# Rows of a modulation, loaded singly and worked off behind the weight splits of a diffusion layer

## The chip, the cores and the metric

The kernel runs on one core of one Trainium2 chip. The metric is the device time of one execution in microseconds (us), lower is better. Three runs of the kernel before gave 2001.37, 2008.41 and 2005.83 us; the median is 2005.83 us.

## What is computed

One layer of a diffusion backbone in float32: 256 latent tokens (`x`) and 256 context tokens, width 2048. Cut to what matters here:

```python
mod_lat = silu(c) @ w_mod + b_mod          # w_mod: 2048 x 12288
sh1, sc1, g1, sh2, sc2, g2 = split(mod_lat, 6)
u = modulate(rmsnorm(h), sh1, sc1) @ w_in  # context and latent tokens
y_ssm = group_rmsnorm(ssd(u) * silu(z), 4 groups)   # state-space half
y_sc  = rmsnorm(bg * conv(cg * hv))                 # short-convolution half
h = x + g1 * (concat(y_ssm, y_sc) @ w_out)
f = modulate(rmsnorm(h), sh2, sc2)
h = h + g2 * expert_choice_ffn(f, w_router, w_gate, w_up, w_down)  # 16 experts
return rmsnorm(h)
```

The first modulation (`sh1`, `sc1`) is needed at once. The later one (`sh2`, `sc2`, `g1`, `g2`, four vectors of 2048) is needed only after the two halves, and its weights are 4 x 2048 x 2048 numbers, 67 MB.

## The kernel before

Every weight of `w_in` and `w_out` goes through the same step, `split_tile`: SP's queue loads a tile of 512 KB (`raw`, three buffers), ScalarE rounds it to the short float format (`whi`, L89), VectorE subtracts this from the original (`wlo`, L90), and TensorE multiplies three times, high by high, high by low and low by high (L326, L329, L765). `whi` and `wlo` have three buffers each, so TensorE can be at most three tiles behind VectorE. There are 241 such tiles: first some for the first chunk of projections, then from about 200 us on the short convolution's first block, four groups of the state-space half (each with a projection of x in banks `g`, its convolution L389/L391, a scan made of L602 to L630, a projection of z, and a norm), three more blocks of the short convolution, and 64 tiles of `w_out`. Then comes the router, and after it 16 experts, whose 402 MB of weights stream through a ring of buffers of 1 MB (`ebig`, `abig`, `mwt`; L934, L960, L981). Three loads of experts stand in SP's queue already among the tiles of `w_in`.

The later modulation isn't done on TensorE. `mod_lat` takes 512 columns at a time: the 16 row blocks of 128 x 512 (256 KB each) are loaded by POOL's queue (`mraw`, L238), and VectorE multiplies each by its 128 values of `c` and adds it to an accumulator (`macc`, L242 for the first, L244 for the other 15). Four transposes on TensorE (`pc`, L250), a reduction and an addition (L251, L252) make 512 values. 16 such columns make the four vectors, 256 rows in all. A load brings two rows (512 KB) into one of two buffers; the last three columns, in the time of `w_out`, load one row (256 KB) into one of two buffers. The table `MODS` says behind which group, block or pass how many columns are written down.

The order of each engine's instructions is set before the launch by a list scheduler that goes by priority, and priority is the place in the program, shifted by hand: weight tiles 300 places earlier (`AHEAD`), columns 250 later (`LATE`), transposes 50 later (`COLS`), the norms of groups 200 later (`NORM`). On the chip each engine then works its own list strictly in order, so that an instruction which waits holds all behind it.

A norm (`rms_bcast`) sums squares over 128 partitions by a product with ones (`pss`, L543), VectorE and POOL take the power -1/2 (`rc`, L545, L546), and a second product spreads it (`pb`, L549). POOL adds the squares beforehand (`sq`, L638, L639).

Of the kernel before, what the change touches and what calls it, by code (L numbers as in the profile page):

```python
# [17 lines left out]

AHEAD = 300
LATE = 250  # L20
NORM = 200
COLS = 50
# [8 lines left out]
MODS = (1, 1, 1, 1, 1, 1, 1, 0, 0, 0, 1, 1, 1, 1, 1, 1, 3, 0, 0, 0)  # L31
# [3 lines left out]
def layer(ctx: ExitStack, tc: tile.TileContext, x, c, cx, c_ctx, w_mod, b_mod, norm_mix_w, w_in,  # L35
# [27 lines left out]
    def sbank(name="s"):  # L63
        return bank("s", 4, name)
# [10 lines left out]

    def raw_tile():
        return wp.tile([P, 2, 512], F32, name="raw", tag="raw", bufs=3)

    def split_tile(src, k0, c0, n, kn):

        with tc.high_priority(offset=ahead[0]):
# [8 lines left out]
            nc.vector.tensor_tensor(lv, wv, hv.bitcast(F32), op=OP.subtract)  # L90
        return hv, lv

# [140 lines left out]
    def mod_lat(c0, dst, pool, kn, bias, paired):  # L233

        acc = pool.tile([P, 512], F32, name="macc", tag="macc", bufs=1)
        for k0 in range(0, KT, kn):
            w = pool.tile([P, kn, 512], F32, name="mraw", tag="mraw", bufs=2)
            nc.gpsimd.dma_start(w, w_mod.rearrange("(k p) c -> p k c", p=P)[:, k0:k0 + kn, c0:c0 + 512])  # L238
            for j in range(kn):
                cs = csl[:, k0 + j:k0 + j + 1]  # L240
                if k0 + j == 0:
                    nc.vector.tensor_scalar(acc, w[:, j], cs, None, op0=OP.mult)  # L242
                else:
                    nc.vector.scalar_tensor_tensor(acc, w[:, j], cs, acc, op0=OP.mult, op1=OP.add)  # L244
        with tc.high_priority(offset=-COLS):
            pc = sbank("pc")
            av = acc.rearrange("p (b c i) -> p b i c", b=2, i=2)
            for j in range(4):
                src = av[:, j // 2, j % 2] if paired else acc[:, P * j:P * j + P]
                nc.tensor.transpose(pc[:, P * j:P * j + P], src, ident)  # L250
            nc.vector.tensor_reduce(dst, pc.rearrange("p (j k) -> p j k", j=4), axis=mybir.AxisListType.X, op=OP.add)  # L251
            nc.vector.tensor_tensor(dst, dst, bias, op=OP.add)  # L252

# [224 lines left out]
    def sc_block(j, gp, dst):  # L478
# [7 lines left out]
        if j:  # L486
            mods_late(8 + 2 * j, gp)
# [30 lines left out]

    mods = const.tile([P, 4, KT], F32, name="mods")
    sh2, G, g1c, g2c = (mods[:, i] for i in range(4))
    late = [(j, q) for j in range(4) for q in range(4)]

    def mod_late(pool=None, kn=2):
        with tc.high_priority(offset=-LATE):
            j, q = late.pop(0)
            dst = mods[:, j, 4 * q:4 * q + 4]
            c0 = (3, 4, 2, 5)[j] * D + 512 * q
            bias = pcol[:, 1 + j, 4 * q:4 * q + 4] if j < 2 else bcol[:, c0 // P:c0 // P + 4]  # L530
            mod_lat(c0, dst, pool or mp, kn, bias, j < 2)
            if j == 1:
                nc.vector.scalar_tensor_tensor(dst, dst, 1.0, nffn[:, 4 * q:4 * q + 4], op0=OP.add, op1=OP.mult)

    def mods_late(i, pool=None, kn=2):
        for _ in range(MODS[i]):
            mod_late(pool, kn)

    def rms_bcast(sq, n):

        pss = sbank("pss")
        for t in range(2):
            nc.tensor.matmul(pss[:, t:t + 1], sq[:, P * t:P * t + P], ones[:, 0:1], start=True, stop=True)  # L543
        rc = const.tile([P, 2], F32, name="rc", tag="rc", bufs=2)
        nc.vector.tensor_scalar(rc, pss[:, 0:2], 1.0 / n, EPS, op0=OP.mult, op1=OP.add)  # L545
        nc.gpsimd.tensor_tensor(rc, rc, mhalf[:, 0:2], op=OP.pow)  # L546
        pb = sbank("pb")
        for t in range(2):
            nc.tensor.matmul(pb[:, P * t:P * t + P], rc[:, t:t + 1].to_broadcast([P, P]), ident, start=True, stop=True)  # L549
        return pb[:, 0:L]  # L550
# [103 lines left out]
    def gate_norm(g):  # L654
# [7 lines left out]
        with tc.high_priority(offset=-NORM):  # L662
            rb = rms_bcast(squares(y32[g]), 512)
            normed(y32[g], rb, nssm[:, 4 * g:4 * g + 4])

    for g in range(NG):
        ssd_group(g)
        mods_late(2 * g)
        gate_norm(g)
        mods_late(2 * g + 1)  # L670
    ssdg.close()
    ssd.close()
    mpool.close()
# [13 lines left out]
    sums = gp.tile([P, L], F32, name="scs")  # L687
    yt = None
    for j in range(1, 4):
# [9 lines left out]
        mods_late(9 + 2 * j, gp)  # L699
    rb = rms_bcast(sums, D)  # L700
    for j in range(4):
        normed(ysc[j], rb, nsc[:, 4 * j:4 * j + 4])
# [4 lines left out]
    g2r = hp_.tile([P, 512], F32, name="g2r")  # L707
# [4 lines left out]
    for j in range(4):  # L712
        ysplit(ysc[j], 4 + j)
    ypool.close()
# [329 lines left out]
```

## Time and profile before

| | us |
|---|---|
| median of three runs | 2005.83 |
| the profiled execution | 1996.63 |
| its span, first to last instruction | 1994.8 |
| TensorE busy | 1651.4 |
| VectorE busy | 900.3 |
| ScalarE busy | 516.6 |
| POOL busy | 143.9 |

Until about 1060 us TensorE is nearly always busy; from then on the 16 DMA engines are, at 420 GB/s, to near the end. Busy time of TensorE is modelled for pipelined matmuls, so a stretch in which it is busy throughout may still hold slow ones; the granted clock stands beside it (1.00 is 2.4 GHz, and at 1.2 GHz it reads 0.50). "Idle before" and "waited for" name what ended a wait last.

### The profile page before, as it was taken

To read this page: it belongs to the slowest core of one execution; us is meant where nothing else is said; L and a number is where in the kernel's file an instruction comes from. 1 tells how busy PE (TensorE), PEld (TensorE's weight loads), DVE (VectorE), ACT (ScalarE), POOL (GpSimd) and SP (SyncE) were. 2 spreads that over 40 slices of the span, in tenths; PEclk is the share of its full clock that TensorE was granted. 3 is DMA by queue.
4 is the path that set the end of the run, shared out by engine and by line. 5 is a ranking of instruction groups with operands and counts; after the bars stand their busy time and mean duration, and the time that the engine had idled before them with its cause. 6 is when DMAs were issued, how large, how long until landed. Compare 5 with 4: busy or idle time off the path is not lost.

```text
span 1994.8 us, 25507 instructions
## 1 busy us (share of the span) xinstructions
PE 1651.4 (83%) x10318; PEld 991.2 (50%) x10318; DVE 900.3 (45%) x1390; ACT 516.6 (26%) x850; POOL 143.9 (7%) x209
## 2 busy tenths in 40 slices
PE   7999999999899989989988766676667676767775
PEld 5677997868698989877872111111111111111122
DVE  2458975867888777886743101111101111111113
ACT  4322574373657333433320000000000000000002
POOL 1001000101121212111200000000000000000000
PEclk9999999999999989999999899989899989888998
DMA  9965654736476888797888999999999999999997
GB/s 354 405 233 145 207 148 115 234 110 218 150 232 197 306 313 290 260 319 260 271 310 365 420 420 420 420 420 420 420 420 420 420 420 420 420 421 420 420 420 276
DMA packets 178086, 641.12 MB, mean 321 GB/s; under 512 B 17549, under 2 KB 50594, under 8 KB 128944
## 3 DMA queue, kind: packets, MB, share of 16 engines
q1 hardware_dynamic: 158496, 570.20, 74.2%
q0 software_dynamic: 19184, 68.24, 11.0%
q8 instruction: 81, 1.33, 0.3%
q10 hardware_dynamic: 288, 1.05, 0.1%
q14 instruction: 37, 0.30, 0.0%
HBM read 637.34 MB, written 2.10 MB: 321 GB/s over the span
## 4 chain that ended last, share of the span: by engine, by line
DMA 58%; PE 22%; issue 9%; DVE 8%; ACT 1%; SPq 1%; POOL 1%; DVEq 0%; POOLq 0%; ACTq 0%
DMA abig<-in_w_up_dram 16%; DMA mwt<-in_w_up_dram 9%; PE g L329 9%; DMA mraw<-in_w_mod_dram 9%; DMA abig<-in_w_down_dram 8%; PE g L326 6%; DMA mwt<-in_w_down_dram 6%; DMA ebig<-in_w_up_dram 5%; DVE macc L244 3%; DVE wlo L90 2%; DMA raw<-in_w_in_dram 2%; DMA ebig<-in_w_down_dram 1%; DMA raw<-in_w_out_dram 1%; PE pm L216 1%; PE s L329 1%
## 5 line engine op out<-in xcount | busy, mean ns | idle before, releaser
L329 PE MATMUL g<-abig,whi 128*128 128x256 f32 x2048 | 376.3, 287 | 15.2 <-ACT whi L89 7.5
L89 ACT CAST whi<-raw 128x1024 fp32r<-128x1024 f32 x241 | 253.9, 1054 | 381.7 <-DMA raw<-in_w_in_dram 92.5
L90 DVE TENSOR_TENSOR wlo<-raw,whi 128x1024 fp32r<-128x1024 f32 x241 | 293.6, 1221 | 102.7 <-ACT whi L89 100.2
L329 PEld LDWEIGHTS g<-abig,whi 128*128 128x128 f32 x2048 | 319.8, 194 | 21.3 <-issue 11.8
L329 PE MATMUL g<-abig,wlo 128*128 128x256 f32 x1024 | 285.7, 288 | 4.7 <-DVE wlo L90 4.6
L940 PE MATMUL gu<-abig,xe 128*32 128x512 f32 x1088 | 202.2, 625 | 78.6 <-DMA abig<-in_w_up_dram 58.1
L244 DVE SCALAR_TENSOR_TENSOR macc<-mraw,csl,macc 128x512 f32<-128x512 f32 x240 | 185.6, 773 | 85.6 <-DMA mraw<-in_w_mod_dram 83.6
L326 PE MATMUL g<-abig,whi 128*128 128x512 f32 (+1 forms) x672 | 213.2, 397 | 2.4 <-ACT abig L310 2.0
L945 DVE SCALAR_TENSOR_TENSOR hid<-hid,gu 64x512 f32<-64x512 f32 x16 | 10.9, 679 | 444.9 <-ACT hid L944 444.9
L944 ACT ACTIVATE hid<-gu 64x512 f32<-64x512 f32 x16 | 9.4, 590 | 765.9 <-PE gu L940 765.9
L329 PEld LDWEIGHTS g<-abig,wlo 128*128 128x128 f32 x1024 | 194.5, 194 | 9.1 <-DVE wlo L90 6.9
L940 PE MATMUL gu<-mwt,xe 128*32 128x512 f32 x616 | 122.5, 629 | 49.9 <-DMA mwt<-in_w_up_dram 37.1
L765 PE MATMUL g<-whi,abig 128*128 128x512 f32 (+1 forms) x640 | 157.6, 350 | 2.6 <-DVE htmp L772 2.2
L940 PEld LDWEIGHTS gu<-abig,xe 128*32 128x32 f32 x1088 | 38.4, 110 | 230.4 <-DMA abig<-in_w_up_dram 101.9
L238 POOL DMA_DIRECT2D mraw<-in_w_mod_dram x152 | 101.1, 665 | 681.0 <-DVE macc L244 475.6
L326 PEld LDWEIGHTS g<-abig,whi 128*128 128x128 f32 (+1 forms) x672 | 122.4, 185 | 38.4 <-issue 8.3
L326 PE MATMUL g<-abig,wlo 128*128 128x512 f32 (+1 forms) x336 | 130.6, 394 | 0.0
L765 PEld LDWEIGHTS g<-whi,abig 128*128 128x128 f32 x640 | 112.5, 191 | 18.8 <-issue 2.5
L974 DVE TENSOR_TENSOR ebig<-ebig,g 128x512 f32<-128x512 f32 x112 | 71.7, 683 | 81.7 <-PE g L970 81.5
L765 PE MATMUL g<-wlo,abig 128*128 128x512 f32 (+1 forms) x320 | 103.3, 355 | 5.0 <-DVE wlo L90 4.5
L963 PE MATMUL yd<-abig,hidT 128*32 128x512 f32 x512 | 74.2, 673 | 34.4 <-DMA abig<-in_w_down_dram 30.2
L940 PE MATMUL gu<-ebig,xe 128*32 128x512 f32 x344 | 73.4, 636 | 28.5 <-DMA ebig<-in_w_up_dram 18.9
(317 smaller groups left out, 1565.5 us busy)
## 6 DMA issues: line engine op xcount, KB each, us to landing
raw<-in_w_in_dram SPq DMA_DIRECT2D x177, 512.0 KB, 4.7
abig<-in_w_up_dram SPq DMA_DIRECT2D x68, 1024.0 KB, 19.9
abig<-in_w_gate_dram SPq DMA_DIRECT2D x68, 1024.0 KB, 19.9
abig<-in_w_down_dram SPq DMA_DIRECT2D x64, 1024.0 KB, 19.9
mraw<-in_w_mod_dram POOLq DMA_DIRECT2D x104, 512.0 KB, 5.0
mwt<-in_w_down_dram SPq DMA_DIRECT2D x43, 1024.0 KB, 19.9
mwt<-in_w_gate_dram SPq DMA_DIRECT2D x39, 1024.0 KB, 19.9
mwt<-in_w_up_dram SPq DMA_DIRECT2D x38, 1024.0 KB, 19.9
```

The source lines that it names most:

```text
L89: nc.scalar.copy(hv, wv)
L90: nc.vector.tensor_tensor(lv, wv, hv.bitcast(F32), op=OP.subtract)
L216: nc.tensor.matmul(pm[32 * q:32 * q + 32, o:o + n], cst[:, k], w[:, k - k0], start=(k < 4), stop=(k >= KT - 4), skip_group_check=True)
L238: nc.gpsimd.dma_start(w, w_mod.rearrange("(k p) c -> p k c", p=P)[:, k0:k0 + kn, c0:c0 + 512])
L244: nc.vector.scalar_tensor_tensor(acc, w[:, j], cs, acc, op0=OP.mult, op1=OP.add)
L326: nc.tensor.matmul(banks[ct][0:ncol], st, a[q][:, kk], start=beg, stop=end)
L329: nc.tensor.matmul(banks[ct // 2][0:ncol, o:o + L], st, a[q][:, kk, L:2 * L], start=beg and ct % 2 == 0, stop=end, skip_group_check=True)
L765: nc.tensor.matmul(ob[nn * t + m], yy[i][:, kk, P * t:P * t + P], w[:, j, n * m:n * m + n], start=(kt == order[0] and pi == 0), stop=(kt = ...
L940: nc.tensor.matmul(gu[32 * q:32 * q + 32], xe[:, k], wt[q // 2][:, 1024 * kk + 512 * (q % 2):1024 * kk + 512 * (q % 2) + 512], start=(k == ...
L945: nc.vector.scalar_tensor_tensor(hid, hid, 1.0, gu[0:64], op0=OP.add, op1=OP.mult)
L963: nc.tensor.matmul(yd[32 * q:32 * q + 32], hidT[:, j, 32 * c2:32 * c2 + 32], t[:, 512 * q:512 * q + 512], start=(kt == 0), stop=(kt == FF ...
L974: nc.vector.tensor_tensor(av, h[:, t, 512 * q:512 * q + 512] if e_ == 0 else av, pc[q], op=OP.add)
```

## The change

The change does five things. A counter (`tick`) goes up by one with each weight tile, and work can be put off by a number of tiles (`at_tick`). The function for a column becomes a generator that yields after every row; behind each tile's subtraction the tile gives out 1.30 rows on average until 192 rows are done (three vectors), and 1.05 in the time of `w_out` until 256. A row is always one load of 256 KB, into one of four buffers (the same memory as two of 512 KB). The reduction after a column's transposes is put off by two tiles. The sums of a norm are put off by three tiles and their spreading by two more; what follows from the last norm, the split of the short convolution's result and the preparation of the router are put off with it. The sum of squares goes into one of the four row buffers, the hand-set shifts of priority are gone, and the memory pool of the rows stays open until the experts.

```diff
-MODS = (1, 1, 1, 1, 1, 1, 1, 0, 0, 0, 1, 1, 1, 1, 1, 1, 3, 0, 0, 0)
+RATE, RATE_OUT = 130, 105
...
-            nc.vector.tensor_tensor(lv, wv, hv.bitcast(F32), op=OP.subtract)
+            sub = nc.vector.tensor_tensor(lv, wv, hv.bitcast(F32), op=OP.subtract)
+        tick[0] += 1
+        with tc.issue_after(sub.ins):
+            for x in sorted(y for y in due if y[0] <= tick[0]):
+                due.remove(x)
+                x[2]()
+            if pace[0]:
+                pace[0]()
...
-            w = pool.tile([P, kn, 512], F32, name="mraw", tag="mraw", bufs=2)
-            nc.gpsimd.dma_start(w, w_mod.rearrange("(k p) c -> p k c", p=P)[:, k0:k0 + kn, c0:c0 + 512])
...
+                for k in range(KT):
+                    w = mp.tile([P, 512], F32, name="mraw", tag="mraw", bufs=4)
+                    nc.gpsimd.dma_start(w, w_mod[P * k:P * k + P, c0:c0 + 512])
+                    cs = csl[:, k:k + 1]
+                    if k == 0:
+                        nc.vector.tensor_scalar(acc, w, cs, None, op0=OP.mult)
+                    else:
+                        nc.vector.scalar_tensor_tensor(acc, w, cs, acc, op0=OP.mult, op1=OP.add)
+                    if k < KT - 1:
+                        yield
...
+                at_tick(2, fin)
+                yield
...
+    def rms_bcast(sq, n, then):
+
+        def sums():
+            pss = sbank("pss")
...
+            def spread():
+                pb = sbank("pb")
...
+                then(pb[:, 0:L])
+            at_tick(2, spread)
+        at_tick(3, sums)
...
-        nc.gpsimd.tensor_tensor(sq[0][:, 0], sq[0][:, 0], sq[0][:, 1], op=OP.add)
-        return sq[0][:, 0]
+        out = mp.tile([P, 512], F32, name="sqs", tag="mraw", bufs=4)[:, 0:L]
+        nc.gpsimd.tensor_tensor(out, sq[0][:, 0], sq[0][:, 1], op=OP.add)
+        return out
...
+    rms_bcast(sums, D, finish_sc)
...
+    at_tick(6, prepare)
```

Three places in the order of instructions. First TensorE in the first pass of `w_out`, where the short convolution's sums (`pss`) and their spreading (`pb`) stand among the weight products, before:

```order
L765 MATMUL g<-whi,abig 128x512 x2
L250 MATMUL pc<-ident,macc 128x128
L543 MATMUL pss<-ones,scs 128x1 x2
L250 MATMUL pc<-ident,macc 128x128 x3
L549 MATMUL pb<-ident,rc 128x128 x2
L726 MATMUL pt<-ident,mods 128x128 x12
L765 MATMUL g<-whi,abig 128x512 x2
```

and now:

```order
L402 MATMUL pc<-ident,macc 128x128 x4
L574 MATMUL pss<-ones,g2r 128x1 x2
L802 MATMUL g<-whi,abig 128x512 x2
L802 MATMUL g<-wlo,abig 128x512 x2
L802 MATMUL g<-whi,abig 128x512 x4
L802 MATMUL g<-wlo,abig 128x512 x2
L802 MATMUL g<-whi,abig 128x512 x4
L802 MATMUL g<-wlo,abig 128x512 x2
L802 MATMUL g<-whi,abig 128x512 x4
L802 MATMUL g<-wlo,abig 128x512 x2
L802 MATMUL g<-whi,abig 128x512 x6
L802 MATMUL g<-wlo,abig 128x512 x2
```

Between sums and spreading there was no weight product; now two and a half tiles of them stand there (the rows go on with `whi` x1 and then `pb`).

Second VectorE in the second group of the state-space half, at the convolution that frees the banks `g` (`cvt` is its scratch, `macc` a row of the modulation), before:

```order
L90 TENSOR_TENSOR wlo<-raw,whi 128x1024
L244 SCALAR_TENSOR_TENSOR macc<-mraw,csl,macc 128x512
L389 SCALAR_TENSOR_TENSOR cvt<-g,col_124,cvt 128x255
L244 SCALAR_TENSOR_TENSOR macc<-mraw,csl,macc 128x512
L391 SCALAR_TENSOR_TENSOR cvt<-g,col_124,cvt 128x255
L389 SCALAR_TENSOR_TENSOR cvt<-g,col_124,cvt 128x4x63
L244 SCALAR_TENSOR_TENSOR macc<-mraw,csl,macc 128x512
L391 SCALAR_TENSOR_TENSOR cvt<-g,col_124,cvt 128x4x63
L244 SCALAR_TENSOR_TENSOR macc<-mraw,csl,macc 128x512
L545 TENSOR_SCALAR rc<-pss 128x2
L90 TENSOR_TENSOR wlo<-raw,whi 128x1024
```

and now (`W`, `ce` and `py` belong to the scan of the group before):

```order
L441 SCALAR_TENSOR_TENSOR cvt<-g,col_124,cvt 128x255
L443 SCALAR_TENSOR_TENSOR cvt<-g,col_124,cvt 128x255
L441 SCALAR_TENSOR_TENSOR cvt<-g,col_124,cvt 128x4x63
L653 TENSOR_TENSOR W<-W,cbm 128x1536
L443 SCALAR_TENSOR_TENSOR cvt<-g,col_124,cvt 128x4x63
L96 TENSOR_TENSOR wlo<-raw,whi 128x1024
L655 TENSOR_TENSOR W<-W 128x4x128
L652 TENSOR_TENSOR ce<-ce,CT 128x1024
L441 SCALAR_TENSOR_TENSOR cvt<-g,col_124,cvt 128x255
L443 SCALAR_TENSOR_TENSOR cvt<-g,col_124,cvt 128x255
L441 SCALAR_TENSOR_TENSOR cvt<-g,col_124,cvt 128x4x63
```

The rows of the modulation no longer stand between the pieces of that convolution. They come later, at places in runs, of which the longest is this one in the same group:

```order
L96 TENSOR_TENSOR wlo<-raw,whi 128x1024
L395 SCALAR_TENSOR_TENSOR macc<-mraw,csl,macc 128x512 x9
L652 TENSOR_TENSOR ce<-ce,CT 128x1024
L395 SCALAR_TENSOR_TENSOR macc<-mraw,csl,macc 128x512
L96 TENSOR_TENSOR wlo<-raw,whi 128x1024
```

Ten rows stand there between two subtractions; in the order before the longest run, in the third group, is of ten as well.

Third POOL's queue around the squares (`sq`) of the first group, before:

```order
L238 DMA mraw<-in_w_mod_dram 128x2x512 x2
L638 TENSOR_TENSOR sq<-sq 128x512
L639 TENSOR_TENSOR sq<-sq 128x256
L238 DMA mraw<-in_w_mod_dram 128x2x512 x6
L546 TENSOR_TENSOR rc<-rc,mhalf 128x2
```

and now:

```order
L390 DMA mraw<-in_w_mod_dram 128x512 x35
L674 TENSOR_TENSOR sq<-sq 128x512
L676 TENSOR_TENSOR sqs<-sq 128x256
L390 DMA mraw<-in_w_mod_dram 128x512 x4
L577 TENSOR_TENSOR rc<-rc,mhalf 128x2
```

Before the first squares 10 loads with 20 rows were issued, now 42 loads with 42 rows; behind them the loads still wait for the squares.

## Rows read from the trace of the kernel before

**Rows 1.** Busy by stretch: PE, PEld, DVE, ACT, POOL; then clock, DMA share, GB/s.

```profile
225.00:340.00 115.00, 115.00 (x803) 101.11 (x802) 81.08 (x112) 74.12 (x137) 2.52 (x2) 1.00 0.49 139
340.00:565.00 225.00, 213.09 (x1238) 173.66 (x1237) 177.60 (x258) 116.62 (x226) 36.88 (x45) 0.98 0.59 183
565.00:640.00 75.00, 74.05 (x568) 65.25 (x568) 60.64 (x78) 51.37 (x105) 9.47 (x12) 1.00 0.68 206
640.00:810.00 170.00, 157.88 (x1267) 154.91 (x1266) 133.78 (x170) 67.22 (x77) 36.78 (x46) 0.97 0.87 294
810.00:1012.00 202.00, 188.25 (x1011) 158.01 (x1010) 150.21 (x189) 77.91 (x90) 37.67 (x64) 0.98 0.83 280
```

**Rows 2.** The chain of waits where the experts begin: start, us, what.

```profile
1058.94 3.67 PE gu L940 x32
1062.61 9.48 DMA ebig<-in_w_down_dram
```

**Rows 3.** Busy by stretch, as in the first group, around the first expert.

```profile
1045.00:1050.00 5.00, 3.70 (x8) 1.44 (x8) 4.73 (x21) 0.58 (x1) 0.00 (x0) 1.00 1.01 419
1055.00:1060.00 5.00, 3.67 (x26) 1.34 (x22) 2.02 (x6) 0.58 (x1) 0.00 (x0) 0.78 0.18 72
1065.00:1070.00 5.00, 5.00 (x52) 1.54 (x48) 0.00 (x0) 0.00 (x0) 0.00 (x0) 1.00 1.01 421
```

**Rows 4.** What TensorE waited for, 340 to 1012 us: total, times, longest.

```profile
PE g L329 <- ACT whi L89: 7.5, 2, 6.3
PE g L329 <- DVE cvt L391: 6.8, 4, 2.5
PE g L329 <- DVE wlo L90: 4.6, 8, 1.3
PE g L765 <- DVE wlo L90: 4.5, 6, 1.1
PE pc L250 <- DVE macc L244: 4.2, 4, 2.4
PE py L629 <- DVE W L619: 2.5, 2, 2.1
PE g L765 <- DVE htmp L772: 2.2, 1, 2.2
PE pb L549 <- POOL rc L546: 1.4, 2, 1.0
```

**Rows 5.** Costliest groups: busy, mean ns | idle before, and what ended it.

```profile
L244 DVE SCALAR_TENSOR_TENSOR macc<-mraw,csl,macc 128x512 f32<-128x512 f32 x240 | 185.6, 773 | 85.6 <-DMA mraw<-in_w_mod_dram 83.6
L238 POOL DMA_DIRECT2D mraw<-in_w_mod_dram x152 | 101.1, 665 | 681.0 <-DVE macc L244 475.6
```

**Rows 6.** What VectorE waited for, 870 to 1012 us: total, times, longest.

```profile
DVE macc L244 <- DMA mraw<-in_w_mod_dram: 34.2, 27, 3.2
```

**Rows 7.** Loads of two rows, 640 to 870 us, issue to landing.

```profile
DMA to landing us min/median/max: 4.1/5.5/9.4
```

**Rows 8.** Loads of one row, 870 to 1012 us, issue to landing.

```profile
DMA to landing us min/median/max: 2.9/4.1/6.7
```

**Rows 9.** POOL's DMA queue, 640 to 810, then 875 to 1006 us: packets, MB, share.

```profile
q0 software_dynamic: 5034, 18.33, 33.8%
...
q0 software_dynamic: 3596, 11.79, 27.8%
```

**Rows 10.** Busy by stretch, as in the first group, around two long waits.

```profile
725.00:735.00 10.00, 3.65 (x22) 3.15 (x22) 1.82 (x2) 2.38 (x3) 0.00 (x0) 0.72 0.79 304
735.00:745.00 10.00, 10.00 (x68) 10.00 (x67) 8.46 (x11) 2.85 (x3) 2.17 (x3) 0.76 0.91 298
865.00:870.00 5.00, 1.62 (x12) 0.95 (x10) 3.74 (x7) 2.09 (x2) 0.81 (x2) 0.94 0.58 216
```

**Rows 11.** SP's queue, 700 to 745 us: start, us, issue.

```profile
713.48 0.46 SPq L934 DMA_DIRECT2D ebig<-in_w_gate_dram  x1
...
716.39 25.23 SPq L84 DMA_DIRECT2D raw<-in_w_in_dram  x7
```

**Rows 12.** What POOL waited for, whole span: total, times, longest.

```profile
POOL sq L638 <- ACT sq L637: 121.4, 5, 114.4
```

More of the change, by code (lines that the diff above doesn't have):

```diff
@@ L19 @@
 AHEAD = 300
-LATE = 250
-NORM = 200
-COLS = 50
 URGENT = 200
@@ L377, in layer, with mod_rows_to, pace_, fn @@
+    steps = mod_rows()
+    n_rows, owed = [0], [0]
+    def mod_rows_to(n):
+        while n_rows[0] < n and next(steps, 0) is None:
+            n_rows[0] += 1
+    def pace_(rate, top):
+        def fn():
+            owed[0] += rate
+            mod_rows_to(min(top, n_rows[0] + owed[0] // 100))
+            owed[0] %= 100
+        return fn
+    pace[0] = pace_(RATE, 12 * KT)
     ssd = ExitStack()
@@ L517, in layer @@
     gp = ssdg.enter_context(tc.tile_pool(name="ssdg", bufs=1, reuse_waits="tile"))
[L521 to L550, printed above, removed]
+    def rms_bcast(sq, n, then):
+        def sums():
+            pss = sbank("pss")
+            for t in range(2):
+                nc.tensor.matmul(pss[:, t:t + 1], sq[:, P * t:P * t + P], ones[:, 0:1], start=True, stop=True)
+            rc = const.tile([P, 2], F32, name="rc", tag="rc", bufs=2)
+            nc.vector.tensor_scalar(rc, pss[:, 0:2], 1.0 / n, EPS, op0=OP.mult, op1=OP.add)
+            nc.gpsimd.tensor_tensor(rc, rc, mhalf[:, 0:2], op=OP.pow)
+            def spread():
+                pb = sbank("pb")
+                for t in range(2):
+                    nc.tensor.matmul(pb[:, P * t:P * t + P], rc[:, t:t + 1].to_broadcast([P, P]), ident, start=True,
+                                     stop=True)
+                then(pb[:, 0:L])
+            at_tick(2, spread)
+        at_tick(3, sums)
     y_hi, y_lo = [None] * 4, [None] * 4
@@ L685, in layer @@
     gp = sp = scx.enter_context(tc.tile_pool(name="sc", bufs=1, reuse_waits="tile"))
-    sums = gp.tile([P, L], F32, name="scs")
+    g2r = hp_.tile([P, 512], F32, name="g2r")
+    sums = g2r[:, 0:L]
     yt = None
@@ L698, in layer @@
                 nc.gpsimd.tensor_tensor(sums, sums, sq, op=OP.add)
[L699 to L702, printed above, removed]
+    mod_rows_to(12 * KT)
+    pace[0] = pace_(RATE_OUT, 16 * KT)
     scx.close()
@@ L743, in layer, with prepare @@
-    nc.vector.tensor_copy(shw, psb[:, 0:NE])
+    shw = hp_.tile([P, NE], F32, name="shw")
+    g1 = []
+    def prepare():
+        g1p = rpool.enter_context(tc.tile_pool(name="g1p", bufs=1, reuse_waits="tile"))
+        g1b = g1p.tile([P, D], F32, name="g1b")
+        g1.append(g1b)
+        for q in range(4):
+            pt = sbank("pt")
+            for j in range(4):
+                k = 4 * q + j
+                nc.tensor.matmul(pt[:, P * j:P * j + P], g1c[:, k:k + 1].to_broadcast([P, P]), ident, start=True, stop=True)
+            nc.scalar.copy(g1b[:, 512 * q:512 * q + 512], pt)
+        nc.gpsimd.memset(gwr, 0.0)
+        for i in range(2):
+            nc.sync.dma_start(wr.rearrange("p (b i) e -> p i b e", i=2)[:, i],
+                              w_router.rearrange("(b p i) e -> p i b e", p=P, i=2)[:, i])
+        psb = sbank("psb")
+        for k in range(KT):
+            nc.tensor.matmul(psb[0:1, 0:NE], sh2[:, k:k + 1], wr[:, k], start=(k == 0), stop=(k == KT - 1))
+        nc.vector.tensor_tensor(wr, wr, G.rearrange("p (k o) -> p k o", o=1).to_broadcast([P, KT, NE]), op=OP.mult)
+        srow = rp.tile([1, NE], F32, name="srow")
+        nc.vector.tensor_copy(srow, psb[0:1, 0:NE])
+        psb = sbank("psb")
+        nc.tensor.matmul(psb[:, 0:NE], ones[0:1, 0:P], srow, start=True, stop=True)
+        nc.vector.tensor_copy(shw, psb[:, 0:NE])
@@ L747, in layer @@
     pq, pl, ns = None, None, 0
-    for pi_, (c0, cn) in enumerate(passes):
-        mods_late(16 + pi_, rp, 1)
+    for c0, cn in passes:
         n = min(cn, 512)
@@ L809, in layer @@
             ns += 1
+    mod_rows_to(16 * KT)
+    flush()
+    rpool.close()
+    rq = rpool.enter_context(tc.tile_pool(name="rq", bufs=1, reuse_waits="tile"))
     rh = const.tile([P, 2], F32, name="rh")
@@ L876, in layer @@
     rpool.close()
+    mpool.close()
     wpool.close()
```

94 lines of the change are left out of this document (40 added, 54 removed).

## The prediction

> **What bounds the kernel now.** I read the busy times by stretch first, then the chain of waits at the end, then what TensorE waits for, and last the row loads. The stretches show TensorE busy 115.00 of 115 us between 225 and 340, and 213.09 of 225, 74.05 of 75, 157.88 of 170 and 188.25 of 202 us after it, while the DMA share stays under 0.9 and VectorE is busy for 70 to 81% of the time [rows 1]. So up to the router the kernel is bound by TensorE, and all that can be won there is its idle time and its slow clock. The idle time from 340 to 1012 us is 11.91 + 0.95 + 12.12 + 13.75 = 38.7 us. The granted clock of those stretches, 0.98, 1.00, 0.97 and 0.98, costs 0.02 x 225 + 0.03 x 170 + 0.02 x 202 = 13.6 us more. The ceiling of any gain is thus about 52 us.
>
> What follows the router moves as a block. The first expert's products begin at 1058.94 us, and from 1062.61 on the chain is a row of weight loads up to the end [rows 2]. Before that the DMA engines run out of work: their share falls from 1.01 to 0.18 between 1055 and 1060 us and is back at 1.01 at 1065 [rows 3]. The buffers for experts are full by then, and the next load needs a product that frees one. So a microsecond won before the router is a microsecond of the whole, and one lost likewise.
>
> **The change part by part.** The work is the same: 256 rows of 0.773 us on VectorE [rows 5], the same transposes and products, the same bytes. 152 loads become 256; a load keeps POOL for 0.665 us [rows 5], which is 69 us more on an engine that is busy for 37 of 225 or 170 us [rows 1] and off the path. What changes is when a row can be had, and what stands in front of what.
>
> *Supply of rows, (a).* VectorE sat idle for 83.6 us before rows whose load had not landed [rows 5], 34.2 us of it between 870 and 1012 [rows 6]. While it waits, the subtractions behind it wait too, and TensorE has at most three tiles in hand. What the buffers can give follows from issue, landing and use. Two buffers of two rows: 0.665 + 5.5 [rows 7] + 2 x 0.773 = 7.7 us for four rows, 1.9 us a row. Two buffers of one row, in the time of `w_out`: 0.665 + 4.1 [rows 8] + 0.773 = 5.5 us for two, 2.8 us a row. Four buffers of one row: 5.5 us for four, 1.4 us a row. The need: a tile takes TensorE 24 matmuls of 157.88 / 1267 = 0.125 us [rows 1], 3.0 us, and the order now puts 74 rows behind 52 tiles of the three later blocks, so one in 2.1 us; in `w_out` it is 73 rows behind 64 tiles in 202 us before, one in 2.8. So the old buffers could just supply that or not quite, and the new ones have a third to spare. TensorE's waits for `wlo` and for the last row ahead of the transposes are 4.6 + 4.5 + 4.2 = 13.3 us [rows 4]. All of it could go, or none if they come from the sheer number of instructions; I take two thirds, 8.9 us, since the waits for rows are most frequent where these waits are.
>
> *Sums given out later, (b).* At the short convolution's sums TensorE stood idle for 3.4 of 5 us [rows 10], with the order showing sums, transposes and spreading back to back. Now two and a half tiles (7.5 us) stand between. Most of that idle time is the wait for the last row (2.4), counted in (a); the wait for the power on POOL is 1.4 us in all [rows 4]. I take 1.0. What is late next: the 16 multiplications and the splits behind the spreading still stand ahead of the next subtractions on VectorE, and there TensorE may wait for a microsecond or two again, which I count in (f).
>
> *Order on VectorE, (c).* Waits for a convolution that frees the banks (6.8), for `W` (2.5) and for `htmp` (2.2) make 11.5 us [rows 4]. In the order, rows between the 66th and the 125th subtraction, which is the time of groups 1 to 3, fall from 94 to 62, because 42 instead of 20 are already done by then; those between the pieces of the convolution are gone. That frees 32 x 0.773 = 25 us on VectorE in a stretch where it was busy for 177.60 of 225. But ScalarE stands in those chains as well, and nothing was done for it. I take a third, 3.8 us (0 to 11.5).
>
> *The tiles behind the expert loads, (d).* At 713.48 us SP issues three loads of 1 MB for experts, and the next weight tile only at 716.39 [rows 11]; TensorE then waits 6.3 of the 7.5 us that it waits for `whi` [rows 4]. The three loads stand at the same place of SP's queue in both orders. Whether TensorE gets through depends on how many split tiles it has in hand, which is 3 x 3.0 = 9 us when VectorE isn't late, as it was here. I take half, 3.7 us (0 to 7.5).
>
> *The clock, (e).* The granted clock falls to the lower level behind the longer waits: 0.72 and 0.76 in the two stretches around that wait [rows 10]. Fewer waits mean fewer falls; I take half of 13.6, 6.8 us.
>
> *New waits, (f).* Between 225 and 340 us no row was worked off, since POOL stood for 114.4 us before the squares of the first group and the loads behind them stood with it [rows 12]. Now 22 more rows fall there or before, 17 us on a VectorE that is busy for 81 of 115 us [rows 1]; it still fits, with little to spare. The sum of squares takes one of the four row buffers until its product is done. And rows still come in runs, below. I take 5 us, bounds 0 to 25.
>
> The sum: 8.9 + 1.0 + 3.8 + 3.7 + 6.8 - 5 = 19.2 us. Against the profiled execution (1996.63 us, of which 1.8 around the span of 1994.8) that gives 1977.4. The three runs lie above it, 2001 to 2008, and no row says where these 9 us are; I take the gain from their median: 2005.8 - 19.2 = 1986.6, so 1987.
>
> One rule speaks against the split of the loads. POOL's queue moved 18.33 MB of two-row loads with 33.8% of 170 us, 3.13 us a MB, and 11.79 MB, nearly all in one-row loads, with 27.8% of 131 us, 3.09 us a MB [rows 9]: single rows cost the DMA engines nothing more. The Trainium skill (DMA: Bandwidth & Descriptors, "Anatomy of one DMA") gives a load from POOL a fixed 2.0 us and the rest by its bytes, and "Measured" there advises batches of 1 MiB. By that, as an estimate from the page, 256 KB would take 2.6 us where 512 KB take 3.2, 1.6 times as much for a MB; the trace does not agree.
>
> **The rivals.** *Rows still come in runs (A).* "One or two rows behind each tile" doesn't hold in the groups: POOL still stands before each group's squares with the loads behind it [rows 12], and the order shows runs of up to ten rows between two subtractions, as before. Then (c) and (d) don't come, and half of (e): 19.2 - 3.8 - 3.7 - 3.4 = 8.3 us, 1997.5. The order speaks for it; the smaller number of rows in the groups against it.
>
> *Nothing to be measured (B).* VectorE still has the same instructions, and each wait removed lets TensorE run into the next one. If of (a) to (e) only half comes, with 8 us of new waits, the gain is 24.2 / 2 - 8 = 4.1 us: 2002. For it: VectorE is at 79% in the groups even without its waits [rows 1].
>
> *Runs that starve TensorE (C), slower.* In a run the first four rows are there, the others come as buffers allow: with one buffer held by the squares, 5.5 / 3 = 1.8 us each. Ten rows then take 4 x 0.773 + 6 x 1.8 = 14 us, in which no tile is split, and TensorE has 9 us in hand. It waits 5 us, and its clock falls, some 2.5 us more (a quarter of 10 us, as in the stretch with 0.76 [rows 10]). The order has five runs of five rows or more in the groups. If all cost this, it is 37 us; against (a) to (e) without (c), 20.4, that is 17 us slower: 2022. It decides once the runs cost more than these 20 us. Against it: the runs before, up to ten rows too, left no wait over 2.5 us in that stretch [rows 4], because TensorE has the scan's products there.
>
> *Single rows cost DMA time (D).* If a one-row load took 1.6 times the DMA time of its bytes, the share of 33.8% would grow by 0.2, the DMA share of that stretch from 0.87 [rows 1] to 1.07, and the 170 us by 12: 2005.8 - 19.2 + 12 = 1999. The cost by MB [rows 9] speaks against it. The rule of the skill is what this rival would be.
>
> **How the numbers follow.** A measurement of this kernel can tell a change of 0.3%, 6 us. The forecast has 0.48, with its own range of 1974 to 1997; A 0.18, B 0.16, C 0.15, D 0.03. Faster by more than 6 us: the forecast, A and D, less 0.02 of A and D that lie within 6 us: 0.67. Within 0.3%: B and those 0.02, 0.18. Slower: C, 0.15. The range is 1966 to 2011: the lower end is the ceiling of 52 us less a quarter that will stay, the upper a C in which two or three runs cost the full price.
>
> **What would show it.** Right for (a): VectorE's idle time before rows falls from 83.6 us to under 35, and TensorE's waits for `wlo` and the last row from 13.3 to about 4. (b): no wait of TensorE for the power. (c): the wait for the convolution falls from 6.8 to about 4. (d): the wait for `whi` after the three expert loads is under 4 us. (e): the clock of the stretches up to the router reads 0.98 or more throughout. The first expert's products begin 15 to 25 us earlier, and from there to the end it takes the same time as before; if that distance changes, the reading of the end as a block is wrong. Wrong in all: TensorE's idle time before the router at 35 us or more, or waits of 3 us and more for `wlo` in the groups behind runs of rows, which would be C.

## The result, and the profile after

The changed kernel takes 1977.8 us (median of 4 runs, 1976.4 to 1980.8), the kernel before 2003.6 in the same series (2000.4 to 2008.4). The ratio is 0.9871 [0.9845, 0.9897]: it is 25.8 us faster. The forecast was 1987 us, in a range of 1966 to 2011, and faster with a chance of 0.67. A second series of the same two kernels gave 1978.5 and 2004.1 us, 0.9872 [0.9849, 0.9895]. The profiled execution of the changed kernel has a span of 1974.6 us, against 1994.8.

The two spans differ by 20.2 us, the medians by 25.8. The traced execution of before took 1996.63 us and lies below every timed run of it (1997.5 to 2010.7 over all series), so what follows explains the 20 us between the traces. For the other 5 or 6 there is no trace.

First the busy time by stretch of the changed kernel (start and end in us; length and busy time of PE, PEld, DVE, ACT, POOL with their counts; then granted clock, DMA share, GB/s). It answers to [rows 1].

```profile
225.00:340.00 115.00, 115.00 (x782) 104.00 (x780) 91.14 (x130) 54.42 (x78) 14.83 (x28) 1.00 0.68 210
340.00:565.00 225.00, 216.89 (x1285) 173.94 (x1284) 171.34 (x243) 136.25 (x284) 38.61 (x59) 0.98 0.49 150
565.00:640.00 75.00, 75.00 (x582) 66.58 (x581) 60.13 (x67) 53.23 (x109) 14.22 (x20) 1.00 0.63 196
640.00:803.00 163.00, 154.43 (x1262) 153.00 (x1261) 137.06 (x179) 64.44 (x71) 51.46 (x83) 0.98 0.92 316
803.00:1012.00 209.00, 200.51 (x1137) 167.91 (x1136) 155.24 (x195) 82.12 (x98) 44.54 (x79) 1.00 0.86 298
```

TensorE's idle time from 340 to 1012 us is now 8.1 + 0 + 8.6 + 8.5 = 25.2 us, where it was 38.7. The clock costs 0.02 x 225 + 0.02 x 163 = 7.8 us, where it was 13.6 (it is printed to two decimals, so each of these products can be off by about 1 us). Those two give 13.5 + 5.8 = 19.3 us. Where the experts begin, the chain of waits (start, us, what), against [rows 2]:

```profile
1037.37 16.50 PE gu L982 x128
```

That is 21.6 us earlier than 1058.94. From there to the end it takes 937.2 us, before 935.9. Next what TensorE waited for from 340 to 1012 us (total, times, longest), against [rows 4]:

```profile
PE g L328 <- ACT whi L95: 7.0, 2, 4.9
PE g L802 <- ACT whi L95: 3.8, 3, 2.1
PE g L802 <- DVE wlo L96: 2.8, 3, 1.7
PE py L665 <- DVE W L655: 2.2, 1, 2.2
PE g L328 <- DVE cvt L443: 2.1, 2, 1.3
PE g L325 <- DVE zt L697: 1.8, 1, 1.8
PE g L328 <- DVE wlo L96: 1.8, 3, 1.0
PE py L665 <- DVE ce L652: 1.5, 2, 0.8
PE g L802 <- DVE htmp L809: 1.0, 1, 1.0
```

The waits for `wlo` have halved, those for the last row ahead of the transposes (4.2 us) and for the power (1.4 us) are gone, that for the convolution fell from 6.8 to 2.1. The wait for `whi` has grown, from 7.5 to 10.8. The rows on VectorE and their loads on POOL, from the page's costliest groups (busy, mean ns | idle before, and what ended it), against [rows 5]:

```profile
L395 DVE SCALAR_TENSOR_TENSOR macc<-mraw,csl,macc 128x512 f32<-128x512 f32 x240 | 185.7, 774 | 31.5 <-DMA mraw<-in_w_mod_dram 29.3
...
L390 POOL DMA_DIRECT2D mraw<-in_w_mod_dram x256 | 137.7, 538 | 586.4 <-DVE macc L395 318.0
```

VectorE's idle time before rows fell from 83.6 to 29.3 us with the duration of a row unchanged. Part of it came back in another place: its idle time before subtractions that wait for ScalarE's rounding rose from 100.2 to 131.0 us. VectorE now waits more for tiles and less for rows.

### The profile page after: what moved, and what is told of

It reads as the page before. It is cut to its first block, busy times and chain, and to the rows that moved or that the text cites. A ratio compares the mean times of both kernels' runs of the same rounds, so it can differ in the third digit from the quotient of the medians.

```text
span 1974.6 us, 25811 instructions
## 1 busy us (share of the span) xinstructions
PE 1645.2 (83%) x10318; PEld 985.4 (50%) x10318; DVE 905.5 (46%) x1390; ACT 514.9 (26%) x850; POOL 184.0 (9%) x313
## 3 DMA queue, kind: packets, MB, share of 16 engines
q0 software_dynamic: 20848, 68.25, 10.1%
q10 hardware_dynamic: 288, 1.05, 0.1%
## 4 chain that ended last, share of the span: by engine, by line
DMA 52%; PE 31%; issue 8%; DVE 4%; ACT 2%; POOL 2%; SPq 1%; POOLq 0%; DVEq 0%; ACTq 0%
DMA abig<-in_w_up_dram 15%; PE g L325 11%; DMA mwt<-in_w_up_dram 9%; DMA abig<-in_w_down_dram 8%; PE g L328 6%; DMA mwt<-in_w_down_dram 6%; PE g L802 5%; DMA ebig<-in_w_up_dram 5%; DMA mraw<-in_w_mod_dram 5%; DMA raw<-in_w_in_dram 1%; PE pm L236 1%; PE s L328 1%; POOL mraw L390 1%; PE gu L982 1%; DMA ebig<-in_w_down_dram 1%
## 5 line engine op out<-in xcount | busy, mean ns | idle before, releaser
L96 DVE TENSOR_TENSOR wlo<-raw,whi 128x1024 fp32r<-128x1024 f32 x241 | 295.6, 1229 | 132.1 <-ACT whi L95 131.0
L395 DVE SCALAR_TENSOR_TENSOR macc<-mraw,csl,macc 128x512 f32<-128x512 f32 x240 | 185.7, 774 | 31.5 <-DMA mraw<-in_w_mod_dram 29.3
L390 POOL DMA_DIRECT2D mraw<-in_w_mod_dram x256 | 137.7, 538 | 586.4 <-DVE macc L395 318.0
```

The costliest lines, as they stand in the source:

```text
L96: sub = nc.vector.tensor_tensor(lv, wv, hv.bitcast(F32), op=OP.subtract)
L390: nc.gpsimd.dma_start(w, w_mod[P * k:P * k + P, c0:c0 + 512])
L395: nc.vector.scalar_tensor_tensor(acc, w, cs, acc, op0=OP.mult, op1=OP.add)
```

## The experiments

Theory S: the supply of rows (single loads in four buffers) brings most of it. Its rivals: N, the late sums; R, the rows' new places; later B (bandwidth), O, P and Q for single stretches; these letters are not those of the prediction's rivals. Every kernel was timed against the kernel before, in 4 to 12 runs.

| kernel | median us | ratio to before, interval | first product of `w_out` | from there to the first expert | from there to the end |
|---|---|---|---|---|---|
| before | 2003.6 | | 815.2 | 243.8 | 935.9 |
| changed | 1977.8 | 0.9871 [0.9845, 0.9897] | 803.7 | 233.7 | 937.2 |
| e1 two-row loads | 2009.4 | 1.0026 [1.0015, 1.0037] | 826.5 | 236.2 | 937.2 |
| e2 sums at once | 1976.7 | 0.9853 [0.9833, 0.9874] | 803.9 | 233.8 | 937.2 |
| e3 before, four singles | 1990.2 | 0.9924 [0.9908, 0.9940] | 809.6 | 245.3 | 937.6 |
| e4 rows not loaded | 1970.3 | 0.9840 [0.9820, 0.9860] | 806.5 | 224.5 | 936.9 |
| e5 expert loads spaced | 1977.5 | 0.9867 [0.9842, 0.9893] | 801.0 | 238.4 | 936.5 |
| e6 rows in the groups | 1983.7 | 0.9891 [0.9875, 0.9907] | 815.9 | 232.6 | 937.2 |
| e10 rows earlier | 1988.4 | 0.9931 [0.9909, 0.9953] | 820.5 | 231.0 | 937.4 |
| e11 router products late | 1979.6 | 0.9890 [0.9869, 0.9910] | 807.0 | 233.4 | 936.0 |
| e12 one pair in `w_out` | 1995.1 | 0.9955 [0.9940, 0.9971] | 804.1 | 252.3 | 937.5 |

The last three columns are from one trace each, in us. The traced executions took 1996.6 (before), 1976.4 (changed), 2001.8 (e1), 1994.4 (e3) and 1987.4 us (e6), so that a column can be some us off what the medians say.

**e1, two rows to a load.** The bytes held are the same, in two buffers instead of four. The sum of squares goes back into `sq`, as before, and takes no row buffer (not shown).

```diff
-                    w = mp.tile([P, 512], F32, name="mraw", tag="mraw", bufs=4)
-                    nc.gpsimd.dma_start(w, w_mod[P * k:P * k + P, c0:c0 + 512])
+                    if k % 2 == 0:
+                        w2 = mp.tile([P, 2, 512], F32, name="mraw", tag="mraw", bufs=2)
+                        nc.gpsimd.dma_start(w2, ...[:, k:k + 2, c0:c0 + 512])
+                    w = w2[:, k % 2]
...
```

> The changed kernel (1977.8 us, against 2003.6 before) with its rows loaded two at a time into two buffers of two rows, as before; the order and the late sums stay. Theory S (the supply of rows brings most: VectorE no longer stands before rows, so splits come in time and the clock stays up): VectorE's idle time before rows goes back from 29 us to 70 or more, TensorE's waits for wlo and for the last row from 4.6 us to about 13, and the time to 1988 to 1996 us. Rival N (the late sums bring most) and rival R (rows worked off earlier and fewer of them in the groups bring most): 1976 to 1983 us, whatever VectorE waits.

2009.4 us: the whole gain goes, and 4.5 us of the time before with it. VectorE's idle time before rows is 58.9 us, less than the 70 expected. What TensorE waited for in that kernel from 340 to 840 us (columns as above):

```profile
PE g L328 <- DVE wlo L96: 8.1, 13, 1.3
PE py L667 <- DVE W L657: 6.9, 1, 6.9
PE g L328 <- ACT whi L95: 5.4, 2, 4.2
PE pss L576 <- POOL sq L677: 5.2, 2, 4.5
PE pb L584 <- POOL rc L579: 2.9, 2, 2.6
```

The waits for `wlo` are back, and with them three that neither kernel had at this size: `W` in the last group, the squares and the power on POOL. N and R predicted no change and fail: the new order with the old loads is slower than the old order. By the table the loss lies ahead of `w_out` (22.8 us), and only 2.5 us in it. That a load of two needs both halves of a buffer free, so that rows come in bursts, is the likely reason; it wasn't tested alone.

**e2, sums at once.**

```diff
-            at_tick(2, spread)
-        at_tick(3, sums)
+            spread()
+        sums()
```

> The changed kernel with the norm's sums and their spreading given out at once instead of three and two tiles later. S and R: TensorE waits about 1.5 us for the power on POOL again and a few more us for the last row and the squares, 1978 to 1982 us. N: the late sums are what keeps VectorE's and TensorE's queues running past the norms, and most of the 26 us go: 1988 to 1998 us.

1976.7 us, not to be told from the changed kernel. N falls. The waits for the power don't even come back; with the rows supplied, no step waits for the norms either way.

**e3, four single-row buffers in the kernel before.**

```diff
-            w = pool.tile([P, kn, 512], F32, name="mraw", tag="mraw", bufs=2)
+            w = pool.tile([P, kn, 512], F32, name="mraw", tag="mraw", bufs=nb)
...
-    def mods_late(i, pool=None, kn=2):
+    def mods_late(i, pool=None, kn=1, nb=4):
```

> The kernel before with its rows up to w_out loaded singly into four buffers, and nothing else (in the time of w_out it had two single-row buffers and keeps them). S: VectorE's idle time before rows falls from 83.6 to about 50 us (the 34 us of w_out stay), TensorE's waits for wlo and the last row up to the router fall by half, and 6 to 12 of the 26 us come: 1991 to 1998 us. N and R: less than 3 us, 2000 to 2004.

1990.2 us: 14.8 us faster than before (2004.9 in that series), by an edit of the rows ahead of `w_out` alone. Its trace took only 2.3 us less than that of before: `w_out` begins 5.6 us earlier, and 1.5 us are lost behind that. Where the other 12 us of the medians are won, no trace shows. Its row group on the page:

```profile
L244 DVE SCALAR_TENSOR_TENSOR macc<-mraw,csl,macc 128x512 f32<-128x512 f32 x240 | 184.9, 771 | 59.1 <-DMA mraw<-in_w_mod_dram 56.8
```

26.8 us of VectorE's idle time have gone, close to the 34 expected. In the table `w_out` is as slow as before, since its two buffers stayed. TensorE's wait for the convolution stays too (340 to 840 us):

```profile
PE g L329 <- DVE cvt L391: 7.3, 4, 2.8
```

**e6, rows back in the groups.**

```diff
-    pace[0] = pace_(RATE, 12 * KT)
...
     for g in range(NG):
+        pace[0] = pace_(250 if g == 0 else 196, 12 * KT)
         ssd_group(g)
...
+        pace[0] = pace_(108, 12 * KT)
         sc_block(j, gp, ...)
```

> The changed kernel with its rows paced as they lay before: none ahead of the first group, 20 in it, 94 in groups 1 to 3, 78 in the later blocks; single loads, four buffers and late sums stay. S: VectorE works off 31 rows more in the groups, but from buffers that keep up: 1977 to 1984 us, and the convolution's wait up by 2 to 4 us. R: the 32 rows (25 us of VectorE) are what made TensorE wait in the groups: the waits from 340 to 565 us go back up by 5 us or more and the time to 1986 to 1995 us. N: 1976 to 1980.

1983.7 us, 4 us given back by the ratios and 6 by the medians: the upper end of S, and below R. The stretch where it happens (columns as in the first table of stretches) and the wait, from 340 to 840 us:

```profile
565.00:640.00 75.00, 67.17 (x488) 58.01 (x487) 63.50 (x84) 46.59 (x98) 15.32 (x29) 0.93 0.69 225
```

```profile
PE py L664 <- DVE W L654: 6.8, 2, 4.0
```

TensorE loses 7.8 us and clock in the last group, where the changed kernel was busy for 75.00 of 75 us. From 340 to 565 us, where R saw the loss, it waits 7.9 us in all, in the changed kernel 8.0, and the convolution is no longer among its waits. In the trace 35, 31 and 32 rows stand behind the 66th to 85th, the 86th to 105th and the 106th to 124th subtraction, about a group each; in the changed kernel 21, 25 and 16, before 37, 37 and 20. So the rows of the first two of these groups cost nothing here. The 4 to 6 us come, through `W`, with 32 rows in the last group, more than the kernel before had there.

**e10, rows earlier still.**

```diff
-    pace[0] = pace_(RATE, 12 * KT)
+    pace[0] = pace_(200, 12 * KT)
...
     for g in range(NG):
+        pace[0] = pace_(RATE, 12 * KT)
...
+        pace[0] = pace_(100, 12 * KT)
         sc_block(j, gp, ...)
```

> The changed kernel with more rows early: two behind each tile ahead of the first group and one behind each tile in the three later blocks. Some 18 rows leave the later blocks, where the DMA share is 0.92 and TensorE waits 7 to 8 us for whi, and stand in group 0. Rival B (bandwidth holds the raw tiles up): the waits for whi in the later blocks fall below 5 us, 1972 to 1975 us. S (the buffers supply enough wherever the rows stand): within 3 us of the changed kernel, 1975 to 1981. Runs of rows that starve TensorE in the groups: waits for W and the convolution there up by 5 us, 1982 us or more.

1988.4 us, 10 us slower than the changed kernel: in time the third of the three expectations. Its waits from 340 to 840 us:

```profile
PE py L665 <- DVE ce L652: 7.3, 2, 5.0
PE g L328 <- ACT whi L95: 6.7, 2, 6.2
PE py L665 <- DVE W L655: 5.8, 3, 2.5
PE pss L574 <- POOL sqs L676: 4.4, 1, 4.4
```

`ce`, `W` and the squares now come late. In the trace 122 rows stand ahead of the 125th subtraction, against 104. But from there to the 177th, in the later blocks, there are still 70, against 74; most of the 18 rows left `w_out` (64 against 78). So the wait for `whi`, which stays, says nothing on B here. Both moves of the rows, later (e6) and earlier, lose.

**e4, no row loads.** All rows read `wone`, one tile loaded once; the squares get a buffer of their own (not shown).

```diff
-                    w = mp.tile([P, 512], F32, name="mraw", tag="mraw", bufs=4)
-                    nc.gpsimd.dma_start(w, w_mod[P * k:P * k + P, c0:c0 + 512])
+                    w = wone
...
```

> The changed kernel without the loads of its rows: all 256 rows on VectorE read one tile that is loaded once (left out: 255 loads of 256 KB, 67 MB, and their issues on POOL). It is the ceiling of what any supply of rows could still give. If four single-row buffers already supply enough, as theory S says, VectorE's 29 us before rows go and TensorE gets little of it: waits for wlo (4.6 us) go, and the time is 1968 to 1974 us with the waits for whi (10.8 us) as before, since they come from the 1 MB expert loads. Rival B (bandwidth: the rows' bytes are what delays the raw tiles, DMA share 0.92 in the later blocks): the waits for whi fall below 4 us, and with the clock that then stays up 1958 to 1968 us. If rows still bound the kernel: below 1955 us.

1970.3 us: without any row loads the kernel is only 8 us faster. By the table these lie in `w_out` (224.5 against 233.7 us); ahead of it nothing is won (806.5 against 803.7). The three later blocks, and what is left of the wait for `whi` from 640 to 1012 us:

```profile
640.00:803.00 163.00, 158.38 (x1301) 157.35 (x1300) 152.19 (x199) 69.26 (x78) 14.58 (x12) 0.99 0.67 201
```

```profile
PE g L328 <- ACT whi L95: 0.2, 1, 0.2
```

The three 1 MB expert loads stand where they stood, and the wait is gone, as B had it and S had not; on the time B was wrong (1958 to 1968 expected) and S right. Weight tiles land in 4.2 us (median, 640 to 803 us) where the changed kernel has 5.7. But the tile behind the expert loads is late here too. ScalarE's roundings before and after that gap (start, us, what, count [idle before, and what ended it]), in the changed kernel and in e4:

```profile
707.68 1.04 ACT L95 CAST whi<-raw 128x1024 fp32r<-128x1024 f32 x1
719.53 1.04 ACT L95 CAST whi<-raw 128x1024 fp32r<-128x1024 f32 x1 [10.82 <-DMA raw<-in_w_in_dram]
```

```profile
718.89 1.05 ACT L95 CAST whi<-raw 128x1024 fp32r<-128x1024 f32 x1 [1.83 <-PE g L328]
727.05 1.05 ACT L95 CAST whi<-raw 128x1024 fp32r<-128x1024 f32 x1 [7.11 <-DMA raw<-in_w_in_dram]
```

That tile took 13.2 us from issue to landing in the changed kernel and 11.4 in e4, and the gap fell from 11.9 to 8.2 us. TensorE ran out of work 8.0 us after the first rounding in the changed kernel and waited 4.9; in e4 it ran out after 9.1 and waited 0.2. How much of this the rows' bytes do, and how much that VectorE and POOL no longer wait for rows, was not tested apart.

**e5, expert loads put apart.** `loads` holds the weight tiles' loads in order.

```diff
+    SPACED = (152, 160, 168, 193, 196, 199, 202)
...
-                nc.sync.dma_start(t.rearrange(...), ...)
+                with tc.issue_after(loads[SPACED[min(nw[0] - 1, 6)]]):
+                    nc.sync.dma_start(t.rearrange(...), ...)
```

> The changed kernel with its first seven expert loads put apart on SP's queue: the first three behind 4, 12 and 20 more weight tiles instead of back to back, the next four three tiles apart in w_out instead of in pairs. If the failed term (d) is right in its mechanism (three loads of 1 MB in a row hold up the next weight tile), the wait of 4.9 us at 720 us goes, the two of 1.3 and 2.1 us in w_out shrink, and the clock of the stretch behind the wait stays up: 5 to 9 us, 1968 to 1973 us. Rival B (bandwidth: the bytes have to be moved in this stretch anyway): the wait comes in pieces elsewhere, 1975 to 1980 us.

1977.5 us, as B had it. The waits from 640 to 1012 us in this kernel, and in the repeated run of the changed one:

```profile
PE g L805 <- DVE wlo L98: 5.1, 3, 3.8
PE g L331 <- ACT whi L97: 5.0, 4, 2.0
PE g L331 <- DVE wlo L98: 3.3, 7, 0.7
PE g L805 <- ACT whi L97: 2.1, 2, 1.9
```

```profile
PE g L328 <- ACT whi L95: 8.1, 2, 6.0
PE g L802 <- ACT whi L95: 3.6, 3, 2.2
PE g L802 <- DVE wlo L96: 2.9, 3, 1.7
...
PE g L328 <- DVE wlo L96: 0.4, 1, 0.4
```

The long wait is gone and 7.1 instead of 11.7 us are spent on `whi`, but 8.4 instead of 3.3 on `wlo`: 15.5 against 15.0 in all.

> The changed kernel itself, as the base for the three beside it on the same chip: by every theory 1975 to 1981 us.

It took 1978.5 us.

**e8, e9, e12, two buffers in `w_out`.** The first two passed over every second buffer; the last gives rows a fixed pair from the 193rd on.

```diff
e8   +                    if 4 * j + q >= 12:
     +                        skip = mp.tile([P, 512], F32, name="skip", tag="mraw", bufs=4)
e9   +                        nc.gpsimd.memset(skip[:, 0:1], 0.0)
e12  -                    w = mp.tile([P, 512], F32, name="mraw", tag="mraw", bufs=4)
     +                    if 4 * j + q < 12:
     +                        w = mp.tile([P, 512], F32, name="mraw", tag="mraw", bufs=4)
     +                    else:
     +                        if not pair:
     +                            pair.extend([mp.tile(...) for _ in range(2)])
     +                        w = pair[k % 2]
```

> The changed kernel with only two of the four row buffers used in w_out (every second buffer is passed over from the 193rd row on); all before it stays. S: VectorE's idle time before rows between 803 and 1012 us goes from 6 us back to 20 or more, w_out takes 5 to 8 us longer than the 210 us from its first product to the last of its fourth pass, 1982 to 1987 us. Rival O (w_out gained from the order of rows, one behind each tile, not from buffers): less than 3 us, 1976 to 1981 us.

> The changed kernel with only two of its four row buffers in w_out, and this time the buffer that is passed over is really taken: POOL writes one column of it behind each load from the 193rd row on (64 writes on an engine that is busy for 45 of 197 us there). S (buffers gave w_out its part): VectorE's idle time before rows between 803 and 1012 us goes from 6 to 20 us or more, the time from the first product of w_out to the first expert from 234 to 240 us or more, 1983 to 1988 us. Rival O (w_out's part came from the order: rows one behind each tile, router's products earlier): less than 3 us, 1976 to 1981.

> The changed kernel with one fixed pair of row buffers from the 193rd row on, so that no more than two rows can be under way in w_out; passing buffers over did not do that. S (four buffers gave w_out and the router their 10 us of the 21.6): VectorE's idle time before rows between 803 and 1012 us goes from 6 to 20 us or more, as in the kernel before with its 42, the time from the first product of w_out to the first expert from 234 to 240 us or more, and 1984 to 1989 us in all. Rival O (they came from the rows' order, one behind each tile): under 3 us, 1976 to 1981 us.

e8 (1978.1 us) and e9 (1978.5) look like O, but the edit did not do what it says. POOL's queue in e8 (start, us, what, how many [idle before, and what ended it]) issues four row loads in one go:

```profile
892.64 2.13 POOL L390 DMA_DIRECT2D mraw<-in_w_mod_dram  x4 [3.84 <-DVE macc L397]
```

Rows whose load is issued and whose use isn't over number three or four for 181 of the 190 us from 810 us on in e8 and for 178 in e9, as in the changed kernel (178), so four buffers were in use. Both say nothing on the question. e12 does: there it is two or fewer for 169 us, and the time is 1995.1 us, 17 us given back. What VectorE waited for from 803 to 1012 us, in e12 and in the changed kernel:

```profile
DVE macc L402 <- DMA mraw<-in_w_mod_dram: 42.5, 32, 4.2
DVE wlo L96 <- ACT whi L95: 14.6, 9, 3.6
```

```profile
DVE wlo L96 <- ACT whi L95: 40.5, 31, 4.5
DVE macc L395 <- DMA mraw<-in_w_mod_dram: 5.8, 6, 1.9
```

Up to 804 us e12 is the changed kernel; then 18.6 us are lost, where the kernel before lost 10.1. O falls. In the changed kernel VectorE waits for the next tile, in e12 for rows, and the next tile waits for it.

**e11, router's products late.**

```diff
+        def route(c0=c0, cn=cn, last=last):
...
+        if last:
+            route()
+        else:
+            held.append(route)
```

> The changed kernel with the router's transposes and products of the first three passes of w_out given out only in the fourth pass, where they stood before (first at the 444th of its product groups, 460th before). Theory P (router): they are what the fourth pass and the router won, 3.8 and 2.9 us, which no term of the forecast held; both come back, 1982 to 1986 us. Rival Q: the work is only moved, what the last pass loses the passes ahead of it win, 1976 to 1980 us.

1979.6 us, not to be told from the changed kernel, as Q had it. Work that is moved out of the last pass is paid for in the passes ahead of it.

## Why the prediction was right, and where it wasn't

**The reading of the bounds** held: the distance from the first expert to the end is 935.9 to 937.6 us in all the kernels, so whatever is won ahead of the router is won in all.

**(a), supply of rows, 8.9 us.** Right in direction and nearly exact on the waits: those for `wlo` and the last row went from 13.3 to 4.6 us. But it was under-sized as a cause. e3 has 14.8 us from it by its medians, e12 takes back 17 us in `w_out`, and e1 shows that without it the change is worth nothing. Each of these prices holds under its own order, so they don't add up to the gain. The term counted only the waits for `wlo` and the last row; late splits also show up as waits for `W`, squares and the power, and as clock. The 4.1 us to landing [rows 8] were too few as well: with four buffers under way single rows landed in 5.2 and 5.0 us (medians, 640 to 797 and 797 to 990 us). And the 0.665 us for the issue of a load [rows 5] is a mean over 104 loads of two rows (0.72 us each) and 48 of one (0.54): the 69 us more on POOL were 36.6 (101.1 to 137.7 us).

**(b), sums later, 1.0 us.** The wait went, as said, but not by this edit: e2 has no such wait either.

**(c), order, 3.8 us.** The waits for the convolution, `W` and `htmp` fell from 11.5 to 5.3 us, against 1.8 more for `zt` and 0.7 for `ce`. The forecast was low. Of its two causes one is borne out, the rows between the pieces of the convolution: that wait is 7.3 us in e3, with the old order and the new supply, 1.6 in e1, with the new order and the old loads, and gone in e6, with the number of rows put back. That number shows a cost only in e6's last group.

**(d), tiles behind the expert loads, 3.7 us.** Wrong: the wait for `whi` rose from 7.5 to 10.8 us. At the place itself, behind the three expert loads, it fell from 6.3 to 4.9 us (6.0 in the repeated run), where the sign asked for under 4. The roundings around that gap in the kernel before:

```profile
720.51 1.05 ACT L89 CAST whi<-raw 128x1024 fp32r<-128x1024 f32 x1 [2.80 <-DMA raw<-in_w_in_dram]
732.11 1.04 ACT L89 CAST whi<-raw 128x1024 fp32r<-128x1024 f32 x1 [10.55 <-DMA raw<-in_w_in_dram]
```

TensorE had more in hand, as the term says: it ran out of work 8.0 us after the first rounding, before 6.4. The step that failed is to count the tiles in hand alone: the next tile came 11.9 us behind the last (before 11.6), more than the 9 us of the forecast. Only in e4, with 8.2, does TensorE get through. The rest of the rise is in places that the term didn't hold: 3.8 us in `w_out`, where the kernel before waited for no `whi`, and 2.0 us at 650 us, where it had 1.2. The DMA share in the later blocks, 640 to 803 us, was 0.88 before and is 0.92 now; e5 shows that putting the expert loads apart wins nothing.

**(e), clock, 6.8 us.** 5.8 by the stretches. What a long wait costs is seen at 720 us, in PE's timeline of the changed kernel (start, us, what, count [idle before, and what ended it]):

```profile
720.63 1.23 PE L328 MATMUL g<-abig,whi 128*128 128x256 f32 x4 [4.93 <-ACT whi L95]
...
724.41 0.63 PE L328 MATMUL g<-abig,whi 128*128 128x256 f32 x2
...
725.37 0.40 PE L328 MATMUL g<-abig,whi 128*128 128x256 f32 x2
```

Behind the wait a pair takes 0.63 us, from 725 us on 0.40. The granted clock of that stretch (columns as in the first table of stretches) is a mean between its lower level and full speed:

```profile
715.00:725.00 10.00, 5.03 (x24) 4.53 (x24) 5.03 (x6) 3.14 (x3) 1.59 (x4) 0.66 0.92 330
```

**(f), new waits, 5 us.** 1.8 us for `zt` and 0.7 for `ce`; the rise of 3.3 in (d) stands there. The first stretch, which the 22 extra rows were to strain, still has TensorE busy for 115.00 of 115 us.

**The sum** of 19.2 us lies beside the 19.3 of the stretches partly by luck: (d) came out 7.0 us worse, and (c), (f) and 2.4 us of small waits that no term held made it good. The 5 or 6 us by which the medians gain more have no trace.

**Not forecast:** 2.9 us between the last product of `w_out` and the first expert's (27.4 to 24.5). e11 shows that moving the products back costs nothing overall, so they aren't a gain of their own.

**The rivals.** A fell: rows do come in runs of up to ten, and POOL waits even longer before the squares (161.6 us, before 121.4), but the gain came all the same. B (nothing measurable) fell. C did not happen here. e10, with 18 rows more in the early groups, loses 10 us, but not quite as C has it: TensorE waits there for `ce`, `W` and the squares, and only 2.8 us for `wlo`. D fell: POOL's queue from 640 to 797 us, against [rows 9],

```profile
q0 software_dynamic: 6000, 19.67, 35.5%
```

is 0.355 x 157 / 19.67 = 2.83 us a MB, where two-row loads had 3.13. The Trainium skill (DMA: Bandwidth & Descriptors, "Anatomy of one DMA") gives each load a fixed part besides its bytes, and puts most of it down to the wait until the last byte is known to have landed. For the time to landing the trace is near that: 4.1 us for 256 KB and 5.5 for 512 KB [rows 8, rows 7] are 1.5 times as much for a MB. The prediction set it against the time of the DMA engines, on which D rests, and that time did not grow.

No version beat the changed kernel: e2 and e5 are within 0.2% of it, their intervals overlap, and e4, which leaves the loads out, is 0.3 to 0.4% faster.

## What to carry over

An engine's idle time before loads, if other work stands behind it in its queue, can be worth more than the waits of the next engine show (here 13.3 us of waits, and 31 us of time between e1 and the changed kernel): make the load as small as what one instruction uses, hold as many under way as issue and landing ask for, and price it by putting the old loads back under the new order. In blocks where the DMA engines were busy for 0.92 of the time, putting loads apart moved a wait and didn't remove it (e5). Before believing an experiment that shows no effect, look in its trace whether the edit did anything (e8, e9), and whether it did so where it was meant to (e10).

## What the runs showed that was not expected

The same 1 MB of buffers (four times 256 KB) was worth 31 us more as four rows than as two pairs (e1 against the changed kernel), though a row costs POOL's DMA queue less, not more, when loaded singly; ahead of `w_out` it was the size of the load that counted, in `w_out` the number of rows under way (two pairs lose 2.5 us there, one pair of single rows 18.6). The issue of a load takes POOL 0.54 us for one row and 0.72 for two.
